# One product over 128 array rows for two terms of each output row, in a 3x3 convolution

## The chip, the cores and the metric

The kernel runs on one core of one Trainium2 chip. The metric is the device time of one execution in microseconds (us); lower is better. Three runs of the kernel before gave 126.46, 126.80 and 128.12 us, so the median is 126.8 us.

## What is computed

A 3x3 convolution with padding 1 over 16 images of 64 channels and 64x64 pixels, to 128 output channels. The weights are masked so that some nine in ten are zero, but the kernel does not use that.

```python
batch, c_in, h, w, c_out, k = 16, 64, 64, 64, 128, 3
x_pad = np.pad(x, ((0, 0), (0, 0), (1, 1), (1, 1)))
for b, co, ci, kh, kw:
    output[b, co] += weight[co, ci, kh, kw] * x_pad[b, ci, kh:kh+h, kw:kw+w]
```

`x` and `weight` are float32 in HBM, and so is the output (33.55 MB). The kernel multiplies in bfloat16 and sums in float32.

## The kernel before

**The arithmetic.** Two output rows, an even row 2r and the odd row 2r+1, share one product. Call the four input rows that they need d0 to d3, and the three rows of the filter g0, g1, g2, each of which stands for its three columns kw. The even row is g0·d0 + g1·d1 + g2·d2, the odd row g0·d1 + g1·d2 + g2·d3. The kernel computes

- P = g1·(d1 + d2), used by both rows,
- E = (g2 - g1)·d2 + g0·d0, so that the even row is P + E,
- O = (g0 - g1)·d1 + g2·d3, so that the odd row is P + O.

**Tiling.** Two images form a pair p (8 pairs). The 64 channels of the first image lie in partitions 0 to 63 and those of the second in 64 to 127. A pair is cut into four blocks of 16 output rows, which makes 32 blocks b; a block has eight even and eight odd rows of both images. A product takes one filter term, one column kw and one image n: it contracts over the 64 partitions of that image and gives 128 output channels by 8 rows by 64 columns (512 elements, or 504 where kw clips the edge). P has 3 columns x 2 images = 6 such matmuls, E and O have 2 terms x 3 columns x 2 images = 12 each, so a block has 30 (L292).

**What each engine does per block.**

- GpSimd (POOL) adds neighbouring rows, `ss` = d1 + d2, a 128x512 tile (L178). It also issues the loads of `x` (L134), which convert to bfloat16 on the way into `xs`.
- ScalarE (ACT) copies the 18 rows that a block needs from `xs` into the window `win` (L211; one 128x1152 copy), and evicts P from PSUM into `pcs` (L219).
- TensorE (PE) runs P, E and O of the block in that order. P waits for `ss` and for `win`; E waits until VectorE has taken the E of the block before out of `ps_e`, and O likewise with `ps_o`.
- VectorE (DVE) adds P + E and P + O into the output tile `os` (L248), two 128x1024 float32 instructions.
- SyncE (SP) stores a finished pair, 4 MB, and the last pair in two halves of 2 MB (L118, L124).

`win`, `ss`, `pcs` and the PSUM tile of P exist twice; `ps_e` and `ps_o` once; the output tile three times. The order of instructions on each engine is the order of the loops that are written out for it, with semaphores between engines (`s`: `ss` ready; `x`: window ready; `p`: P done; `q`: E or O done; `c`: ACT's copies; `e`, `o`: VectorE's sums; `r`: VectorE's marks).

**Head.** Weights are cast into `w_bf`, turned by nine matmuls against an identity (L267), and copied or subtracted into `wT`, which holds five filter rows: g0, g1, g2, g2 - g1, g0 - g1. Seven idle matmuls of 128 rows come before that and seven after it (L262). The first 32 rows of pair 0 arrive as float32 in `x_head`.

Of the kernel before, what the change touches and what calls it, by code (L numbers as in the profile page):

```python
# [12 lines left out]
G0, G1, G2, G21, G01 = range(5)  # L13
# [4 lines left out]
def kernel(  # L18
# [5 lines left out]
):  # L24

# [27 lines left out]
    win = tiles(2, [128, 18, W], BF16, "win")  # L53
# [7 lines left out]
    w_bf = pool.tile([C_OUT, 3, 4 * C_IN], BF16, name="w_bf")  # L61
    wT = pool.tile([128, 5, 3, C_OUT], BF16, name="wT")
# [24 lines left out]
    w_bf4 = w_bf.rearrange("o g (k i) -> o g k i", k=4)  # L87

    def cast_w(copy, g, a, b):
        k = 3 * g + a % 3  # L90
        return copy(out=w_bf4[:, g, a:b, :], in_=w_v[:, k : k + b - a, :])  # L91
# [5 lines left out]
    def tap(g, kw, n):  # L97
        return wT[64 * n : 64 * n + 64, g, (kw - n) % 3, :]

# [4 lines left out]
    HEAD_R, HEAD_C, HEAD_Q = 8, 4, 3  # L104
    R_OF = {p: HEAD_R + p + 1 for p in range(NP - 1)}

    with tc.tile_critical(no_gpsimd_drain=True):  # L107
        with nc.Block(no_gpsimd_drain=True) as block:  # L108
# [22 lines left out]
            def _(gp):  # L131
                def load(p, a, b, *waits):
# [5 lines left out]
                gp.memset(ident, 0.0).then_inc(S("s"), 1)  # L138
# [10 lines left out]
                    ("s", 1),  # L149
                ).then_inc(S("s"), 1)  # L150
# [13 lines left out]
                for b in range(NB):  # L164
                    p, r0 = b // 4, 16 * (b % 4)
                    waits = []
                    if b == 0:
                        waits.append(("xh", 16))
                    if b == 2 or (b % 4 == 0 and b):
                        waits.append((x_sem(p), X_LANDS[p]))  # L170
                    if b >= 2:
                        waits.append(("p", b - 1))
                    if b < 2:
                        src = x_head[:, r0 : r0 + 16, :]
                    else:
                        src = xs[:, p, r0 + 1 : r0 + 17, :]
                    after(
                        gp.tensor_tensor(  # L178
                            out=ss[b % 2], in0=src[:, 0:16:2, :], in1=src[:, 1:16:2, :], op=ADD
                        ),  # L180
                        *waits,
                    ).then_inc(S("s"), 1)
                    if b in AT:
                        load(*AT[b])

            @block.scalar
            def _(act):
                after(cast_w(act.copy, G1, 3, 4), ("w", 16)).then_inc(S("c"), 1)
                cast_w(act.copy, G2, 0, 3).then_inc(S("c"), 1)
                after(act.copy(out=wT[:, G1], in_=wps(G1)), ("q", 1)).then_inc(S("c"), 1)  # L190
                after(act.copy(out=wT[:, G2], in_=wps(G2)), ("q", 3)).then_inc(S("c"), 1)

                def window(b):
                    p, r0 = b // 4, 16 * (b % 4)
                    parts = [(xs[:, p, r0 : r0 + 18, :], 0, [])]
                    if b == 0:
                        parts = [(x_head[:, 0:17, :], 1, [("xh", 16)])]
                    elif b == 1:
                        parts = [
                            (x_head[:, 15:32, :], 0, []),  # L200
                            (xs[:, 0, 33:34, :], 17, [(x_sem(0), X_LANDS[0])]),
                        ]
                    elif b == 2:
                        parts = [(x_head[:, 31:32, :], 0, []), (xs[:, 0, 33:50, :], 1, [])]
                    elif b % 4 == 0:
                        parts[0][2].append((x_sem(p), X_LANDS[p]))
                    if b >= 2:
                        parts[0][2].append(("q", HEAD_Q + 2 * (b - 2) + 2))
                    for k, (src, a, waits) in enumerate(parts):
                        copy = after(  # L210
                            act.copy(out=win[b % 2][:, a : a + src.shape[1], :], in_=src), *waits  # L211
                        )
                        if k == len(parts) - 1:
                            copy.then_inc(S("x"), 1)

                window(0)
                window(1)
                for b in range(NB):
                    after(act.copy(out=pcs[b % 2], in_=ps_p[b % 2]), ("p", b + 1)).then_inc(S("c"), 1)  # L219
                    if b + 2 < NB:  # L220
                        window(b + 2)

            @block.vector
            def _(dve):
                dve.memset(idle_rhs, 0.0).then_inc(S("r"), 1)  # L225
                dve.memset(xs[:, :, 0 : H + 2 : H + 1, :], 0.0)
                dve.memset(win[0][:, 0:1, :], 0.0).then_inc(S("r"), 1)
                after(cast_w(dve.tensor_copy, G1, 0, 3), ("w", 16)).then_inc(S("r"), 1)
                cast_w(dve.tensor_copy, G0, 0, 3)
                cast_w(dve.tensor_copy, G0, 3, 4).then_inc(S("r"), 1)  # L230
                cast_w(dve.tensor_copy, G2, 3, 4).then_inc(S("r"), 1)
                after(dve.tensor_copy(out=wT[:, G0], in_=wps(G0)), ("q", 2)).then_inc(S("r"), 1)  # L232
                after(
                    dve.tensor_tensor(out=wT[:, G01], in0=wps(G0), in1=wT[:, G1], op=SUB), ("c", 3)
                ).then_inc(S("r"), 1)
                after(
                    dve.tensor_tensor(out=wT[:, G21], in0=wps(G2), in1=wT[:, G1], op=SUB), ("c", 4)
                ).then_inc(S("r"), 1)
                for b in range(NB):
                    p, r0 = b // 4, 16 * (b % 4)  # L240
                    for k, src in enumerate((ps_e, ps_o)):
                        waits = [("q", HEAD_Q + 2 * b + k + 1)]
                        if k == 0:
                            waits.append(("c", HEAD_C + b + 1))
                            if b % 4 == 0 and p >= N_O:
                                waits.append((f"st{p % N_O}", 16 * (p // N_O)))
                        after(
                            dve.tensor_tensor(  # L248
                                out=os[p % N_O][:, :, r0 + k : r0 + 16 : 2, :], in0=src, in1=pcs[b % 2], op=ADD
                            ),  # L250
                            *waits,
                        ).then_inc(S("eo"[k]), 1)
                    if b % 4 == 3 or b == NB - 3:
                        dve.memset(mark, 0.0).then_inc(S("r"), 1)

            @block.tensor
            def _(pe):
# [7 lines left out]
                def transposed(g, *waits):  # L265
                    for j in range(3):
                        mm = pe.matmul(  # L267
                            wps(g)[:, j, :], w_bf[:, g, C_IN * j : C_IN * (j + 2)], ident, start=True, stop=True
                        )
                        if j == 0:  # L270
                            after(mm, *waits)
                        if j == 2:
                            mm.then_inc(S("q"), 1)

                keep_busy(7, ("r", 1))
                pe.wait_ge(S("s"), 2)
                pe.sem_inc(S("s"), -2)
                transposed(G1, ("r", 3), ("c", 1))
                transposed(G0, ("r", 4))
                transposed(G2, ("r", 5), ("c", 2))  # L280
# [3 lines left out]
                pe.wait_ge(S("r"), HEAD_R)  # L284

                def product(dst, terms, name, waits):
                    todo = [(t, kw) for t in terms for kw in KW_ORDER]
                    for i, ((src, g, first, step), kw) in enumerate(todo):
                        c_lo, c_hi = max(0, 1 - kw), min(W, W + 1 - kw)
                        for n in range(2):  # L290
                            q = slice(64 * n, 64 * n + 64)
                            mm = pe.matmul(  # L292
                                dst[:, n, :, c_lo:c_hi],
                                tap(g, kw, n),
                                src[q, first : first + 7 * step + 1 : step, c_lo + kw - 1 : c_hi + kw - 1],
                                start=(i == 0),
                                stop=(i == len(todo) - 1),
                            )
                            if n == 0 and i == 0:
                                after(mm, *waits)  # L300
                            if n == 1 and i == len(todo) - 1:
                                mm.then_inc(S(name), 1)

                with pe.Fori(0, NB // TURN, 1):
                    for l in range(TURN):
                        xw = win[l]
                        product(ps_p[l], [(ss[l], G1, 0, 1)], "p", [("s", l + 1), ("x", l + 1)])
                        product(ps_e, [(xw, G21, 2, 2), (xw, G0, 0, 2)], "q", [("e", l + 1)])
                        product(ps_o, [(xw, G01, 1, 2), (xw, G2, 3, 2)], "q", [("o", l + 1)])
                    for name in ("s", "x", "e", "o"):  # L310
                        pe.sem_inc(S(name), -TURN)
# [36 lines left out]
```

## Time and profile before

The profiled execution took 126.21 us in all; the span in its trace is 124.4 us, so 1.81 us lie around the span.

| | us | share of the span |
|---|---|---|
| profiled execution | 126.21 | |
| its span | 124.4 | |
| PE busy | 109.6 | 88% |
| PEld (weight loads) busy | 49.1 | 39% |
| DVE busy | 79.2 | 64% |
| ACT busy | 69.3 | 56% |
| POOL busy | 43.0 | 35% |
| HBM traffic, read and written | 17.07 MB and 33.55 MB | 407 GB/s over the span |

A matmul's busy time overlaps that of its neighbours, so "PE busy" says that something was in the array, not that it was at its peak. PEld is TensorE's loading of weights. In the groups of instructions the columns are: line, engine, operation, output<-input, shape and count, then busy time in us and mean ns of one instruction, then the engine's idle time before them with what ended most of it.

### The profile page before, as it was taken

What the parts mean: (1) busy time and instruction counts of PE and PEld (TensorE: products, weight loads), DVE (VectorE), ACT (ScalarE), POOL (GpSimd) and SP (SyncE); (2) the same over time, 40 slices, a digit from 0 to 9 for tenths busy, and PEclk for the clock granted to TensorE, in tenths of its full rate; (3) what the DMA queues carried; (4) which work ended last, traced back from release to release, by engine and by line L of the source; (5) the groups of instructions that cost most, each with busy time, mean ns of one, the idle gap of its engine ahead of it and who ended that gap; (6) DMA issues with size and microseconds to landing.
All of it is one profiled execution on the core that took longest, in us unless ns stands there. A gap on an engine that the chain in (4) does not pass through costs nothing.

```text
span 124.4 us, 2437 instructions
## 1 busy us (share of the span) xinstructions
PE 109.6 (88%) x983; PEld 49.1 (39%) x983; DVE 79.2 (64%) x83; ACT 69.3 (56%) x71; POOL 43.0 (35%) x48
## 2 busy tenths in 40 slices
PE   5949999999999999999999999999999999992000
PEld 1414444444444444444444444444444444440000
DVE  2615676777677777777777767775867677775000
ACT  4564666666666666666666666657566666630000
POOL 5564333533353334433343334333333333000000
PEclk9999999999999999999999999999999999999855
DMA  3999999999999999999999999999999999999991
GB/s 85 375 225 213 211 219 219 239 438 338 332 363 432 308 329 324 387 353 345 298 379 408 321 369 427 413 367 348 433 421 432 427 384 427 458 390 416 413 419 71
DMA packets 4179, 42.79 MB, mean 344 GB/s; under 512 B 336, under 2 KB 336, under 8 KB 1104
## 3 DMA queue, kind: packets, MB, share of 16 engines
q1 hardware_dynamic: 2736, 34.90, 67.3%
q0 software_dynamic: 1440, 7.86, 30.6%
q14 instruction: 3, 0.02, 0.0%
HBM read 17.07 MB, written 33.55 MB: 407 GB/s over the span
## 4 chain that ended last, share of the span: by engine, by line
PE 84%; DMA 5%; POOL 1%; DVE 1%; SPq 0%; issue 0%; DVEq 0%
PE ps_e L292 33%; PE ps_o L292 33%; PE ps_p L292 17%; DMA x_head<-in_x_dram 5%; POOL s L178 1%; DVE o L248 1%; SPq L112 0%; SPq L343 0%; SPq L107 0%; DVEq L108 0%
## 5 line engine op out<-in xcount | busy, mean ns | idle before, releaser
L248 DVE TENSOR_TENSOR o<-ps_e,pc 128x1024 f32<-128x1024 f32 x32 | 39.2, 1225 | 31.2 <-ACT pc L219 22.9
L178 POOL TENSOR_TENSOR s<-xs 128x512 bf16<-128x512 bf16 x30 | 34.5, 1150 | 58.0 <-PE ps_p L292 58.0
L211 ACT COPY win<-xs 128x1152 bf16<-128x1152 bf16 (+2 forms) x31 | 34.7, 1121 | 34.2 <-PE ps_o L292 34.2
L292 PE MATMUL ps_e<-win,wT 64*128 64x504 bf16 (+1 forms) x384 | 46.8, 377 | 0.0
L292 PE MATMUL ps_o<-win,wT 64*128 64x504 bf16 (+1 forms) x384 | 46.8, 377 | 0.0
L248 DVE TENSOR_TENSOR o<-ps_o,pc 128x1024 f32<-128x1024 f32 x32 | 38.9, 1216 | 0.1
L219 ACT COPY pc<-ps_p 128x1024 f32<-128x1024 f32 x32 | 32.2, 1006 | 1.8 <-PE ps_p L292 1.8
L292 PEld LDWEIGHTS ps_o<-win,wT 64*128 64x128 bf16 x384 | 18.9, 94 | 22.6 <-DVE o L248 0.2
L292 PEld LDWEIGHTS ps_e<-win,wT 64*128 64x128 bf16 x384 | 18.8, 94 | 22.8 <-DVE o L248 0.8
L292 PE MATMUL ps_p<-s,wT 64*128 64x504 bf16 (+1 forms) x192 | 26.0, 377 | 1.6 <-POOL s L178 1.6
L292 PEld LDWEIGHTS ps_p<-s,wT 64*128 64x128 bf16 x192 | 9.4, 94 | 13.2 <-POOL s L178 2.1
L262 PE MATMUL ps_p<-idle_rhs 128*128 128x512 bf16 x14 | 4.8, 503 | 1.4 <-DVE idle_rhs L225 1.4
L134 POOL DMA_DIRECT2D xs<-in_x_dram x10 | 5.7, 573 | 1.0 <-SPq L107 1.0
L211 ACT CAST win<-x_head 128x1088 bf16<-128x1088 f32 (+1 forms) x3 | 2.3, 811 | 2.8 <-PE ps_o L292 1.6
L178 POOL TENSOR_TENSOR s<-x_head 128x512 bf16<-128x512 f32 x2 | 2.5, 1270 | 2.4 <-DMA x_head<-in_x_dram 2.4
L262 PEld LDWEIGHTS ps_p<-idle_rhs 128*128 128x128 bf16 x14 | 1.5, 117 | 3.4 <-DVE idle_rhs L225 1.4
L91 DVE CAST w_bf<-w_sb 128x192 bf16<-128x192 f32 (+1 forms) x4 | 1.1, 348 | 2.0 <-DMA w_sb<-in_weight_dram 2.0
L91 ACT ACT_TABLE_LOAD x1 | 1.3, 1283 | 0.9 <-SPq L107 0.9
L91 ACT CAST w_bf<-w_sb 128x64 bf16<-128x64 f32 (+1 forms) x2 | 0.7, 415 | 1.7 <-DMA w_sb<-in_weight_dram 1.7
L225 DVE MEMSET idle_rhs<- 128x256 uint32 x1 | 0.3, 272 | 1.1 <-SPq L107 1.1
L232 DVE CAST wT<-ps_e 128x384 bf16<-128x384 f32 x1 | 0.6, 557 | 0.3 <-PE ps_e L267 0.3
L190 ACT CAST wT<-ps_o 128x384 bf16<-128x384 f32 x1 | 0.5, 478 | 0.3 <-PE ps_o L267 0.3
(18 smaller groups left out, 5.4 us busy)
## 6 DMA issues: line engine op xcount, KB each, us to landing
out_dram<-o SPq DMA_DIRECT2D x7, 4096.0 KB, 17.3
xs<-in_x_dram POOLq DMA_DIRECT2D x5, 1024.0 KB, 16.3
out_dram<-o SPq DMA_DIRECT2D x2, 2048.0 KB, 10.3
xs<-in_x_dram POOLq DMA_DIRECT2D x3, 512.0 KB, 13.4
x_head<-in_x_dram SPq DMA_DIRECT2D x1, 1024.0 KB, 5.8
xs<-in_x_dram POOLq DMA_DIRECT2D x1, 640.0 KB, 14.2
xs<-in_x_dram POOLq DMA_DIRECT2D x1, 384.0 KB, 21.2
w_sb<-in_weight_dram SPq DMA_DIRECT2D x1, 288.0 KB, 2.9
```

The costliest lines, as they stand in the source:

```text
L91: return copy(out=w_bf4[:, g, a:b, :], in_=w_v[:, k : k + b - a, :])
L134: gp.dma_start(out=xs[:, p, a + 1 : b + 1, :], in_=pair(p)[:, a:b, :]), *waits
L178: gp.tensor_tensor(out=ss[b % 2], in0=src[:, 0:16:2, :], in1=src[:, 1:16:2, :], op=ADD),
L190: after(act.copy(out=wT[:, G1], in_=wps(G1)), ("q", 1)).then_inc(S("c"), 1)
L211: act.copy(out=win[b % 2][:, a : a + src.shape[1], :], in_=src), *waits
L219: after(act.copy(out=pcs[b % 2], in_=ps_p[b % 2]), ("p", b + 1)).then_inc(S("c"), 1)
L225: dve.memset(idle_rhs, 0.0).then_inc(S("r"), 1)
L232: after(dve.tensor_copy(out=wT[:, G0], in_=wps(G0)), ("q", 2)).then_inc(S("r"), 1)
L248: dve.tensor_tensor(out=os[p % N_O][:, :, r0 + k : r0 + 16 : 2, :], in0=src, in1=pcs[b % 2], op=ADD),
L262: mm = pe.matmul(idle_ps, idle_rhs[:, 0:128], idle_rhs, start=True, stop=True)
L292: mm = pe.matmul(dst[:, n, :, c_lo:c_hi], tap(g, kw, n), src[q, first : first + 7 * step + 1 : step, c_lo + kw - 1 : c_hi + kw - 1], start ...
```

## The change

E is now one product per column and image over all 128 partitions instead of two over 64: the window of image n holds d0 in one half of the partitions and, in the other half, the rows two further down, so that the array itself adds g0·d0 + (g2 - g1)·d2. O works in the same way, with (g0 - g1)·d1 and g2·d3. P stays as it was, in pairs of 64-row matmuls. A block has 6 + 6 + 6 = 18 matmuls.

`win[l]` becomes 128 x 2 images x 16 rows x 64, and is filled by four copies of 64 partitions x 1024 per block (`fill`; `upper` names the half of the partitions that is written, n the image):

- GpSimd: image 0, lower half
- VectorE: image 0, upper half (the source lies in partitions 0 to 63, the destination in 64 to 127)
- ScalarE: image 1, lower half (from 64 to 127 into 0 to 63) and image 1, upper half

E's first image now waits for the copies of GpSimd and VectorE, its second for both of ScalarE; P no longer waits for a window. On GpSimd the copy stands between the block's row sum and the load that may follow; on VectorE behind the two sums of the block two earlier; on ScalarE around the eviction of P.

In the head, `wT` holds three sets instead of five; the differences are taken when the weights are cast, and two subtractions from PSUM go. The row sums of blocks 0 and 1 move from GpSimd to VectorE.

```diff
-    win = tiles(2, [128, 18, W], BF16, "win")
+    win = tiles(2, [128, 2, 16, W], BF16, "win")
...
+    def fill(copy, b, n, upper, name):
+        p, r0 = b // 4, 16 * (b % 4)
+        src = slice(64 * n, 64 * n + 64)
+        dst = slice(64 * upper, 64 * upper + 64)
+        first = r0 - 1 + 2 * upper
...
+            if b >= 2 and k == 0:
+                waits.append(("q", HEAD_Q + 2 * (b - 2) + 2))
+            inst = after(copy(out=win[b % 2][dst, n, q : q + rows.shape[1], :], in_=rows), *waits)
+            if k == len(parts) - 1:
+                inst.then_inc(S(name), 1)
...
             @block.gpsimd
                 for b in range(NB):
...
+                    if b >= 2:
+                        waits = [("p", max(b - 1, 2))]
+                        if b == 2 or b % 4 == 0:
+                            waits.append((x_sem(p), X_LANDS[p]))
+                        after(row_sum(gp, b, xs[:, p, r0 + 1 : r0 + 17, :]), *waits).then_inc(S("s"), 1)
+                    fill(gp.tensor_copy, b, 0, 0, "xg")
                     if b in AT:
                         load(*AT[b])
...
             @block.scalar
-                window(0)
-                window(1)
+                fill(act.copy, 0, 1, 1, "xa")
+                fill(act.copy, 0, 1, 0, "xa")
+                fill(act.copy, 1, 1, 1, "xa")
                 for b in range(NB):
                     after(act.copy(out=pcs[b % 2], in_=ps_p[b % 2]), ("p", b + 1)).then_inc(S("c"), 1)
+                    if b + 1 < NB:
+                        fill(act.copy, b + 1, 1, 0, "xa")
                     if b + 2 < NB:
-                        window(b + 2)
+                        fill(act.copy, b + 2, 1, 1, "xa")
...
             @block.vector
+                for b in range(2):
+                    after(row_sum(dve, b, x_head[:, 16 * b : 16 * b + 16, :]), ("xh", 16)).then_inc(S("s"), 1)
+                    fill(dve.tensor_copy, b, 0, 1, "xd")
                 for b in range(NB):
...
+                    if b + 2 < NB:
+                        fill(dve.tensor_copy, b + 2, 0, 1, "xd")
...
             @block.tensor
+                    halves = [slice(64 * n, 64 * n + 64) for n in range(2)]
+                    if g == MID:
+                        order = [(kw, n, halves[n]) for kw in KW_ORDER for n in range(2)]
+                    else:
+                        order = [(kw, n, slice(0, 128)) for n in range(2) for kw in KW_ORDER]
...
-                        product(ps_p[l], [(ss[l], G1, 0, 1)], "p", [("s", l + 1), ("x", l + 1)])
-                        product(ps_e, [(xw, G21, 2, 2), (xw, G0, 0, 2)], "q", [("e", l + 1)])
-                        product(ps_o, [(xw, G01, 1, 2), (xw, G2, 3, 2)], "q", [("o", l + 1)])
+                        product(ps_p[l], lambda n: ss[l], MID, [[("s", l + 1)], []], "p")
+                        product(ps_e, lambda n: win[l][:, n, 0:16:2, :], EVEN,
+                            [[("e", l + 1), ("xg", l + 1), ("xd", l + 1)], [("xa", 2 * l + 2)]], "q")
+                        product(
+                            ps_o, lambda n: win[l][:, n, 1:16:2, :], ODD, [[("o", l + 1)], []], "q"
+                        )
```

More of the change, by code (lines that the diff above doesn't have):

```diff
@@ L11 @@
 SUB = mybir.AluOpType.subtract
-G0, G1, G2, G21, G01 = range(5)
+MID, EVEN, ODD = range(3)
 KW_ORDER = (1, 0, 2)
@@ L60 @@
     idle_rhs = pool.tile([128, 512], BF16, name="idle_rhs")
-    w_bf = pool.tile([C_OUT, 3, 4 * C_IN], BF16, name="w_bf")
-    wT = pool.tile([128, 5, 3, C_OUT], BF16, name="wT")
+    w_bf = pool.tile([C_OUT, 3, 3, 2, C_IN], BF16, name="w_bf")
+    wT = pool.tile([128, 3, 3, C_OUT], BF16, name="wT")
     mark = pool.tile([128, 1], FP32, name="mark")
@@ L86, with w_row @@
     w_v = w_sb.rearrange("o (i k) -> o k i", k=KH * KW)
[L87 to L91, printed above, removed]
+    def w_row(kh):
+        return w_v[:, 3 * kh : 3 * kh + 3, :]
     def wps(g):
@@ L95, in wps @@
         return flat[:, 0:384].rearrange("p (k c) -> p k c", k=3)
-    def tap(g, kw, n):
-        return wT[64 * n : 64 * n + 64, g, (kw - n) % 3, :]
     def x_sem(p):
@@ L103, with row_sum @@
     X_LANDS = {0: 16, 1: 16, 2: 16, 3: 16, 4: 32, 5: 32, 6: 32, 7: 48}
-    HEAD_R, HEAD_C, HEAD_Q = 8, 4, 3
+    HEAD_R, HEAD_C, HEAD_Q = 6, 5, 3
     R_OF = {p: HEAD_R + p + 1 for p in range(NP - 1)}
+    def row_sum(eng, b, rows):
+        return eng.tensor_tensor(out=ss[b % 2], in0=rows[:, 0:16:2, :], in1=rows[:, 1:16:2, :], op=ADD)
+    def fill(copy, b, n, upper, name):
[3 more added lines that the diff above has]
+        first = r0 - 1 + 2 * upper
+        parts = []
+        if p == 0 and first < HEAD:
+            a, z = max(first, 0), min(first + 16, HEAD)
+            parts.append((x_head[src, a:z, :], a - first))
+        if p or first + 16 > HEAD:
+            a, z = (first, first + 16) if p else (max(first, HEAD), first + 16)
+            parts.append((xs[src, p, a + 1 : z + 1, :], a - first))
+        for k, (rows, q) in enumerate(parts):
+            waits = []
+            if b == 0:
+                waits.append(("xh", 16))
+            if b == 1 and k == 1:
+                waits.append((x_sem(0), X_LANDS[0]))
+            if b and b % 4 == 0:
+                waits.append((x_sem(p), X_LANDS[p]))
[4 more added lines that the diff above has]
+                inst.then_inc(S(name), 1)
     with tc.tile_critical(no_gpsimd_drain=True):
@@ L137, in _ @@
                 load(0, HEAD, H)
-                gp.memset(ident, 0.0).then_inc(S("s"), 1)
+                gp.memset(ident, 0.0).then_inc(S("id"), 1)
                 after(
@@ L148, in _ @@
                     ),
-                    ("s", 1),
-                ).then_inc(S("s"), 1)
+                    ("id", 1),
+                ).then_inc(S("id"), 1)
                 for p in range(1, 4):
@@ L165, in _ @@
                     p, r0 = b // 4, 16 * (b % 4)
[L166 to L170, printed above, removed]
-                    if b >= 2:
[L172 to L182, printed above, removed]
+                    if b >= 2:
+                        waits = [("p", max(b - 1, 2))]
+                        if b == 2 or b % 4 == 0:
+                            waits.append((x_sem(p), X_LANDS[p]))
+                        after(row_sum(gp, b, xs[:, p, r0 + 1 : r0 + 17, :]), *waits).then_inc(S("s"), 1)
+                    fill(gp.tensor_copy, b, 0, 0, "xg")
                     if b in AT:
@@ L187, in _ @@
             def _(act):
[L188 to L214, printed above, removed]
@@ L216, in _ @@
-                window(0)
-                window(1)
+                after(act.copy(out=w_bf[:, MID, :, 1, :], in_=w_row(1)), ("w", 16)).then_inc(S("c"), 1)
+                act.copy(out=w_bf[:, EVEN, :, 0, :], in_=w_row(0)).then_inc(S("c"), 1)
+                act.copy(out=w_bf[:, ODD, :, 1, :], in_=w_row(2)).then_inc(S("c"), 1)
+                after(act.copy(out=wT[:, MID], in_=wps(MID)), ("q", 1)).then_inc(S("c"), 1)
+                after(act.copy(out=wT[:, ODD], in_=wps(ODD)), ("q", 3)).then_inc(S("c"), 1)
@@ L226, in _ @@
                 dve.memset(xs[:, :, 0 : H + 2 : H + 1, :], 0.0)
[L227 to L238, printed above, removed]
+                dve.memset(win[0][0:64, :, 0:1, :], 0.0).then_inc(S("r"), 1)
+                after(dve.tensor_copy(out=w_bf[:, MID, :, 0, :], in_=w_row(1)), ("w", 16)).then_inc(S("r"), 1)
+                for g, half, a, b in ((EVEN, 1, 2, 1), (ODD, 0, 0, 1)):
+                    dve.tensor_tensor(
+                        out=w_bf[:, g, :, half, :], in0=w_row(a), in1=w_row(b), op=SUB
+                    ).then_inc(S("r"), 1)
+                after(dve.tensor_copy(out=wT[:, EVEN], in_=wps(EVEN)), ("q", 2)).then_inc(S("r"), 1)
+                for b in range(2):
+                    after(row_sum(dve, b, x_head[:, 16 * b : 16 * b + 16, :]), ("xh", 16)).then_inc(S("s"), 1)
+                    fill(dve.tensor_copy, b, 0, 1, "xd")
                 for b in range(NB):
@@ L265, in transposed @@
                 def transposed(g, *waits):
[L266 to L270, printed above, removed]
+                    for kw in range(3):
+                        src = w_bf[:, g, kw].rearrange("o h i -> o (h i)")
+                        mm = pe.matmul(wps(g)[:, kw, :], src, ident, start=True, stop=True)
+                        if kw == 0:
                             after(mm, *waits)
-                        if j == 2:
+                        if kw == 2:
                             mm.then_inc(S("q"), 1)
                 keep_busy(7, ("r", 1))
[L276 to L280, printed above, removed]
+                pe.wait_ge(S("id"), 2)
+                transposed(MID, ("r", 3), ("c", 1))
+                transposed(EVEN, ("r", 4), ("c", 2))
+                transposed(ODD, ("r", 5), ("c", 3))
                 keep_busy(7)
@@ L284, in _ @@
                 pe.wait_ge(S("r"), HEAD_R)
-                def product(dst, terms, name, waits):
-                    todo = [(t, kw) for t in terms for kw in KW_ORDER]
-                    for i, ((src, g, first, step), kw) in enumerate(todo):
-                        c_lo, c_hi = max(0, 1 - kw), min(W, W + 1 - kw)
[L290 to L302, printed above, removed]
+                pe.wait_ge(S("c"), HEAD_C)
@@ new lines, in product @@
+                def product(dst, src, g, waits, name):
+                    halves = [slice(64 * n, 64 * n + 64) for n in range(2)]
[3 more added lines that the diff above has]
+                        order = [(kw, n, slice(0, 128)) for n in range(2) for kw in KW_ORDER]
+                    for i, (kw, n, q) in enumerate(order):
+                        c_lo, c_hi = max(0, 1 - kw), min(W, W + 1 - kw)
+                        mm = pe.matmul(
+                            dst[:, n, :, c_lo:c_hi],
+                            wT[q, g, kw, :],
+                            src(n)[q, :, c_lo + kw - 1 : c_hi + kw - 1],
+                            start=(kw == KW_ORDER[0]),
+                            stop=(kw == KW_ORDER[-1]),
+                        )
+                        if kw == KW_ORDER[0]:
+                            after(mm, *waits[n])
+                        if i == 5:
+                            mm.then_inc(S(name), 1)
@@ L304, in _ @@
                 with pe.Fori(0, NB // TURN, 1):
                     for l in range(TURN):
-                        xw = win[l]
-                        product(ps_p[l], [(ss[l], G1, 0, 1)], "p", [("s", l + 1), ("x", l + 1)])
-                        product(ps_e, [(xw, G21, 2, 2), (xw, G0, 0, 2)], "q", [("e", l + 1)])
-                        product(ps_o, [(xw, G01, 1, 2), (xw, G2, 3, 2)], "q", [("o", l + 1)])
-                    for name in ("s", "x", "e", "o"):
-                        pe.sem_inc(S(name), -TURN)
+                        product(ps_p[l], lambda n: ss[l], MID, [[("s", l + 1)], []], "p")
@@ new lines, in _ @@
+                        product(
+                            ps_e,
+                            lambda n: win[l][:, n, 0:16:2, :],
+                            EVEN,
+                            [
+                                [("e", l + 1), ("xg", l + 1), ("xd", l + 1)],
+                                [("xa", 2 * l + 2)],
+                            ],
+                            "q",
+                        )
+                        product(
+                            ps_o, lambda n: win[l][:, n, 1:16:2, :], ODD, [[("o", l + 1)], []], "q"
+                        )
@@ L313 @@
+                    for name, n in (("s", 1), ("xa", 2), ("xd", 1), ("xg", 1), ("e", 1), ("o", 1)):
+                        pe.sem_inc(S(name), -n * TURN)
     sixteen = nc.sync.to_reg(16)
```

## The prediction

> **What bounds the kernel now.** I read the chain of waits first. It is TensorE without a break, from 8.59 to 112.65 us; one block reads:
>
> ```profile
> 60.63 0.65 PE ps_p L292 x6
> 61.28 1.30 PE ps_e L292 x12
> 62.58 1.30 PE ps_o L292 x12
> 63.87 0.65 PE ps_p L292 x6
> ```
>
> (start, length, what). A block takes 63.87 - 60.63 = 3.24 us, and 32 of them 103.7. The costliest groups say what one matmul is:
>
> ```profile
> L292 PE MATMUL ps_e<-win,wT 64*128 64x504 bf16 (+1 forms) x384 | 46.8, 377 | 0.0
> ...
> L219 ACT COPY pc<-ps_p 128x1024 f32<-128x1024 f32 x32 | 32.2, 1006 | 1.8 <-PE ps_p L292 1.8
> ...
> L292 PEld LDWEIGHTS ps_e<-win,wT 64*128 64x128 bf16 x384 | 18.8, 94 | 22.8 <-DVE o L248 0.8
> ```
>
> Each lasts 377 ns, but 30 fit into 3.24 us, 108 ns apiece: the two images' 64-row matmuls run side by side, a pair every 3.24/15 = 216 ns. The groups between 5.3 and 7.1 us, then the timeline, show what one full-height matmul costs, by the idle ones of the head:
>
> ```profile
> L262 PE MATMUL ps_p<-idle_rhs 128*128 128x512 bf16 x7 | 1.7, 379 | 0.0
> L262 PEld LDWEIGHTS ps_p<-idle_rhs 128*128 128x128 bf16 x7 | 0.6, 98 | 0.6
> ```
>
> ```profile
> 5.32 1.67 PE L262 MATMUL ps_p<-idle_rhs 128*128 128x512 bf16 x7
> ```
>
> Seven in 1.67 us, the last lasting 0.379: (1.67 - 0.379)/6 = 215 ns each. So a 128-row matmul costs what a pair of 64-row ones costs.
>
> Last the end. The stores' time to landing from 107 us on, and their issues in the timeline:
>
> ```profile
> 113.95 0.37 SPq L124 DMA_DIRECT2D out_dram<-o  x1
> ```
>
> ```profile
> DMA to landing us min/median/max: 9.5/10.3/11.1
> ```
>
> From 113 us on the only store left takes 9.5, so the last half lands at 113.95 + 9.5 = 123.5, and the half issued at 107.53 at 107.53 + 11.1 = 118.6. The last 2.1 MB land 4.9 us after the half before, 430 GB/s, the rate of the last slices of the page (413 to 458). So the last store queued: the DMA engines are a second bound. The HBM line adds up to 17.07 + 33.55 = 50.6 MB, 117.7 us at 430 GB/s, of a 124.4 us span with busy share 9 in nearly every slice. Nothing that only shortens PE's work can take out much over 2 us.
>
> **The change part by part.**
>
> *Matmuls.* Before: 15 pairs x 216 ns. After: 3 pairs of P, and 12 of 128 rows at 215. Again 3.24 us. The 12 fewer matmuls save nothing.
>
> *Weight loads.* 18 per block instead of 30, of 94 or 98 ns. The idle matmuls carry one each at a pitch of 215, so a 128-row load hides under the matmul before: 0. The Trainium skill ("TensorE: Matmul & The Clock Gate", The mechanism) says that a load overlaps a running matmul only where the row groups differ. By that rule the idle pitch would hold the 98 ns too, which the 215 contradicts; the row decides, and the rule is the last rival.
>
> *Going between 64 and 128 rows.* This is new: P to E and O to P, twice a block, 64 times (the first P follows a gap). Inside the loop of before every matmul has 64 rows, and no dense sequence in the trace mixes heights, so it must be bounded. Low: 0, what a change of weights and bank costs now; a gain is excluded because the array accepts no more columns per time in either form (216 and 215). High: the array empties and the next load waits too, 377 - 216 + 98 = 259 ns. Between: it empties but the load hides, 377 - 216 = 161 ns. I take 161: in a pair the two halves of the array work on different matmuls, in a 128-row one on the same, so one may have to be done with before the other begins, and 161 is what the trace has for a matmul whose end nothing overlaps. 2 x 0.161 = 0.32 us a block, 10.3 in 32. The Trainium skill ("TensorEngine Tiling (Array Packing)", Key Properties) states that changing the tiling mode drains TensorE, and gives no price; no run here shows it.
>
> *ACT.* The 1152-element window copy goes (1.15 us; with 1088 elements 1.09, so 0.92 ns per element), two of 1024 come, about 1.03 each. Successive copies start some 0.09 earlier than they end (60.67 + 1.15, next at 61.73), so a block is 2 x 0.94 + 1.01 = 2.9 of 3.24 us. Queue: fill of b+2 at O's end, P's eviction, fill of b+1. The eviction is ready 0.1 us sooner than now. Cost 0; cover left 0.3 us.
>
> *DVE.* 2.43 of 3.24 us busy; it adds a 64x1024 bf16 copy between two SBUF tiles, which the trace lacks. Low: MEMSET of 128x512 words, the same bytes, 0.485. High: the 128x1024 sum from PSUM, 1.225. I take 0.485, nearest in memory and bytes: 2.92, hidden. At 1.225 with overlaps of 0.08 it is 3.42, and 0.18 x 32 = 5.8 us show. Queued behind it is the next P + E sum, which idles 0.8 to 0.9 us for P's eviction today, and behind that the next E, which needs `ps_e`.
>
> *POOL.* 1.15 us a block; it adds a 1024-element copy. Low 1.15 (the row sum reads 2 x 512), high 2.3 (it writes 512): 2.3 or 3.45 us. I take 1.15, for the elements read: hidden. The loads behind the copy are issued some 2.6 us later (after O of two blocks back instead of P); they land 20 us or more before use, so 0.
>
> *Head.* `ss` of block 0 moves to DVE: the 384-element sum took 0.55, so 512 some 0.65 to 0.7 against 1.28, and P starts 0.6 us earlier. But ACT now has four copies (1024, 960, 960, 64 elements, about 2.9 us) before it evicts P of block 0, near 10.1 instead of 9.45; the sum ends near 12.4, and E of block 1 starts there instead of 12.65. Net gain 0.2, and hidden by the queue of stores. Two subtractions fewer end before `x_head` lands at 7.2: 0.
>
> *Sum.* PE ends at 112.65 + 10.3 = 122.95; the sum and issue take 113.95 - 112.65 = 1.3; the last store goes out at 124.25. Alone it needs 4.9 us plus a start: the 0.29 MB of weights took 2.9 from issue to landing, 0.7 of it at 430 GB/s, so 2.2. It lands at 131.35 rather than 123.5: the queue of today, 9.5 - 7.1 = 2.4 us, absorbs part. With 124.4 - 123.5 = 0.9 of span behind it and the 1.81 around the span: 134.1 us, against the profiled 126.21 (0.6 below the median of the runs).
>
> **The rivals.** *Not slower: the change of height is free* or costs little. For it: the pair and the single matmul have the same pitch, and each product's first matmul today changes weights, bank and waits without a bubble. Against: the trace has never seen the two mixed. PE then ends where it did, and DMA ends the span: 126.2. It decides below the point where 2% (2.5 us) show behind the 2.4 of queue: 4.9/64 = 77 ns. Bounds 125.6 (the head's 0.6) to 128.7.
>
> *A helper takes over the bound.* DVE at 1.225: 126.2 + 5.8 - 2.4 = 129.6. POOL at 2.3: 3.45 - 3.24 = 0.21 x 32 = 6.7, so 130.5. Or the two hold each other up: POOL starts its copy at O's end and the next row sum 1.15 later, so DVE's copy, wanted 1.3 after O's end behind P + O, would wait for 2.3, end at 2.8, and the next sum at 4.0, against E's start at 3.89: 0.1 x 32 = 3.5, so 127.3. For it: DVE and ACT lose most of their spare time; against: all the nearest rows fit. That a VectorE copy in a two-port mode and a GpSimd instruction shut each other out is in the Trainium skill ("SBUF — State Buffer", Who interferes with whom); no run here shows it.
>
> *The weights' loads show*: 12 x 98 ns x 32 = 37.6 - 2.4, 161 us. The idle matmuls speak against it.
>
> *Faster by over 2%*: 123.7 or less. Only if stores overlap better than now; the busy share leaves no room.
>
> **How the numbers follow.** Changes of height over 77 ns: 46 in 100 (forecast, 134.1; its own range 129 to 140.4, the latter at 259 ns: 16.6 - 2.4). Free or cheaper: 37. A helper: 12, of which 2 stay inside 2%. Loads: 1. Faster: 4. So faster 0.04, same 0.39, slower 0.57; the 2% stand for what a measurement of this kernel can tell from no change. The range has to reach both: from 125.6, the low bound of the free case, to 136 (190 ns a change), leaving out some 15.
>
> **What would show it.** In the chain of the changed kernel, a block of 3.56 us, with a gap of some 0.16 in front of each first P and first E matmul, and the last store landing 7 us after issue: forecast. Blocks of 3.24 and the last store still in a queue: free. E's idle ended by DVE or POOL copies: helper. The forecast is wrong if P, E and O follow one another at 0.65, 1.30 and 1.30 us.

## The result, and the profile after

The changed kernel takes 133.34 us (median of 4 runs, 133.25 to 136.69) against 126.63 of the kernel before on the same chip: a ratio of 1.050, with a 95% interval of 1.041 to 1.059. The forecast was 134.1, slower. Some executions of a kernel stand a few per cent above the rest, here the highest of the four; ratios leave them out, and where a profile below is of one (experiments 1 and 2), its extra time lies ahead of the second block. Its profiled execution took 133.27 us, with a span of 131.5: 7.1 us more than before.

The chain of waits, first in a stretch where TensorE is alone on it, then around one where it is not (start, length, what):

```profile
96.24 0.75 PE ps_p L289 x6
97.00 1.40 PE ps_e L289 x6
98.40 1.30 PE ps_o L289 x6
99.69 0.75 PE ps_p L289 x6
```

```profile
69.54 0.71 DVE win L129
70.26 0.95 issue
71.21 1.24 DVE o L242
72.44 0.05 issue
72.49 1.47 PE ps_e L289 x6
```

A block takes 99.69 - 96.24 = 3.45 us instead of 3.24. P went from 0.65 to 0.75 and E from 1.30 to 1.40, O kept its 1.30: a piece holds the gap in front of it, so the loss stands in front of P and in front of E, where 64 and 128 rows meet. In the second stretch E waits for VectorE's sum, and that sum for VectorE's own copy into the window.

The costliest groups among the new and altered ones, with busy time and mean ns, then idle time in front:

```profile
L129 ACT COPY win<-xs 64x1024 bf16<-64x1024 bf16 (+2 forms) x61 | 62.7, 1028 | 13.7 <-PE ps_o L289 13.7
L129 POOL COPY win<-xs 64x1024 bf16<-64x1024 bf16 (+1 forms) x30 | 30.8, 1027 | 34.0 <-PE ps_o L289 34.0
...
L129 DVE COPY win<-xs 64x1024 bf16<-64x1024 bf16 (+1 forms) x31 | 31.0, 1000 | 0.9
...
L289 PEld LDWEIGHTS ps_p<-s,wT 64*128 64x128 bf16 x192 | 6.8, 94 | 17.8 <-issue 12.7
```

ScalarE's copy is what the forecast took (1.03), GpSimd's is a little under its low bound (1.03 for 1.15), VectorE's is twice what it took (1.00 for 0.485). The last line is the change of height from the side of the weight loads: 12.7 us in which P's first loads waited for nothing that the profile shows, 0.42 us in each of 30 blocks, of which 0.12 is the usual gap between two loads (216 - 98 ns).

The end of the kernel, by stages: the columns are the stretch, its length, then each engine's busy time and count, the granted clock, the DMA engines' busy share and GB/s.

```profile
100.00:106.80 6.80, 6.80 (x40) 2.55 (x36) 6.67 (x6) 5.88 (x7) 4.18 (x5) 1.00 0.91 386
106.80:109.30 2.50, 2.50 (x16) 1.01 (x13) 2.43 (x5) 2.48 (x3) 2.01 (x2) 1.00 0.00 0
109.30:111.00 1.70, 1.70 (x12) 0.49 (x11) 1.70 (x2) 1.26 (x2) 0.88 (x1) 1.00 0.72 308
111.00:130.00 19.00, 9.41 (x48) 3.55 (x46) 9.26 (x11) 6.09 (x7) 2.29 (x3) 0.87 0.99 414
```

For 2.5 us the DMA engines have nothing to do: in the kernel before the stores always queued here (a share of 0.96 to 1.00 from 88 to 114 us), now the queue runs dry in front of the store of pair 6. That store goes out at 109.25 and takes 11.3 us to land; the two halves of the last pair follow it at 4.9 us each, since each is issued (at 115.5 and 121.7) while the store before it is still under way. 109.25 + 11.3 + 2 x 4.9 = 130.4, and the span ends at 131.5.

### The profile page after: what moved, and what is told of

The parts are those of the page before. It is cut to its first block, busy times and chain, and to the rows that moved or that the text cites. A ratio compares the mean times of both kernels' runs of the same rounds, so it can differ in the third digit from the quotient of the medians.

```text
span 131.5 us, 1819 instructions
## 1 busy us (share of the span) xinstructions
PE 116.9 (89%) x599; PEld 43.9 (33%) x599; DVE 113.7 (86%) x115; ACT 99.5 (76%) x104; POOL 74.0 (56%) x79
## 4 chain that ended last, share of the span: by engine, by line
PE 40%; DVE 27%; issue 12%; ACT 9%; DMA 4%; SPq 0%; DVEq 0%
DVE o L242 19%; PE ps_e L289 17%; PE ps_o L289 16%; DVE win L129 8%; PE ps_p L289 7%; ACT win L129 6%; DMA x_head<-in_x_dram 4%; ACT pc L213 2%; SPq L138 0%; SPq L350 0%; DVEq L242 0%; SPq L133 0%; DVEq L134 0%
## 5 line engine op out<-in xcount | busy, mean ns | idle before, releaser
L129 ACT COPY win<-xs 64x1024 bf16<-64x1024 bf16 (+2 forms) x61 | 62.7, 1028 | 13.7 <-PE ps_o L289 13.7
L129 POOL COPY win<-xs 64x1024 bf16<-64x1024 bf16 (+1 forms) x30 | 30.8, 1027 | 34.0 <-PE ps_o L289 34.0
L289 PE MATMUL ps_e<-win,wT 128*128 128x504 bf16 (+1 forms) x192 | 47.0, 381 | 1.6 <-DVE o L242 1.0
L289 PE MATMUL ps_o<-win,wT 128*128 128x504 bf16 (+1 forms) x192 | 46.8, 380 | 0.0
L129 DVE COPY win<-xs 64x1024 bf16<-64x1024 bf16 (+1 forms) x31 | 31.0, 1000 | 0.9
L289 PEld LDWEIGHTS ps_e<-win,wT 128*128 128x128 bf16 x192 | 16.2, 97 | 30.8 <-DVE o L242 11.1
L289 PEld LDWEIGHTS ps_o<-win,wT 128*128 128x128 bf16 x192 | 18.8, 98 | 22.7 <-DVE o L242 0.6
L289 PEld LDWEIGHTS ps_p<-s,wT 64*128 64x128 bf16 x192 | 6.8, 94 | 17.8 <-issue 12.7
L129 ACT CAST win<-x_head 64x1024 bf16<-64x1024 f32 (+2 forms) x5 | 4.3, 861 | 0.7 <-DMA x_head<-in_x_dram 0.6
L129 POOL CAST win<-x_head 64x960 bf16<-64x960 f32 (+2 forms) x3 | 3.4, 1141 | 2.3 <-DMA x_head<-in_x_dram 2.3
```

The costliest lines, as they stand in the source:

```text
L129: inst = after(copy(out=win[b % 2][dst, n, q : q + rows.shape[1], :], in_=rows), *waits)
L289: mm = pe.matmul(dst[:, n, :, c_lo:c_hi], wT[q, g, kw, :], src(n)[q, :, c_lo + kw - 1 : c_hi + kw - 1], start=(kw == KW_ORDER[0]), stop=(k ...
```

## The experiments

Two theories from the first reading. "Height": each change between 64 and 128 rows costs TensorE a fixed time. "Helpers": the copies that were added on GpSimd, VectorE and ScalarE lengthen the block. The runs below take one away and leave the other. Times are medians; ratios are to the kernel before on the same chip, with 95% intervals.

### 1. The change of height alone

The kernel before, all other engines untouched. Only E and O are multiplied as in the changed kernel.

```diff
-                    todo = [(t, kw) for t in terms for kw in KW_ORDER]
...
+                    if tall:
+                        todo = [(terms[n], kw, n, slice(0, 128)) for n in range(2) for kw in KW_ORDER]
...
```

> The kernel before, with its window, its ScalarE copy and all its other engines untouched; only the 12 pairs of E and O become 12 matmuls of 128 rows, term 0 for the first image and term 1 for the second (the sums over the terms are left out, so that the number of array slots stays 15 a block). Theory 'height': each change between 64 and 128 rows costs TensorE some 106 ns, so a block takes 3.24 + 0.21 = 3.45 us with no further stall, PE ends near 112.6 + 6.7 = 119.3, the store of pair 6 goes out some 5.9 us later, and the time is about 131 us (ratio 1.035 to 1.04). Rival 'helpers': the added copies on GpSimd, VectorE and ScalarE are what lengthens the block; they are absent here, so the block stays at 3.24 and the time at 126.5.

Measured: 131.11 us, ratio 1.039 (1.035 to 1.043). The chain of waits of this run:

```profile
61.24 0.75 PE ps_p L294 x6
62.00 1.40 PE ps_e L294 x6
63.40 1.30 PE ps_o L294 x6
64.70 0.76 PE ps_p L294 x6
```

A block of 64.70 - 61.24 = 3.46 us with none of the copies. "Height" holds, and alone it is worth some 5 us.

### 2. The copies alone

The changed kernel with 64-row matmuls in pairs for E and O.

```diff
-                        order = [(kw, n, slice(0, 128)) for n in range(2) for kw in KW_ORDER]
+                        order = [(kw, n, halves[n]) for _ in range(2) for kw in KW_ORDER for n in range(2)]
...
```

> The changed kernel with all its copies, waits and its head, but E and O multiplied in pairs of 64-row matmuls as before (each image's own half of the partitions, twice; the other half's term is left out). Theory 'height': the block returns to 3.24 us, apart from stalls of 0.26 us in about one block of four where VectorE's copy comes behind GpSimd's; 126 to 127.5 us. Rival 'helpers': the copies are still there, so the block stays near 3.45 and the time near 133.

Measured: 131.2 us, ratio 1.038 (1.033 to 1.044). I had expected 126 to 127.5. So the copies alone cost as much as the changes of height alone. The timeline of this run (start, length, engine, line, operation) shows how:

```profile
63.23 0.42 DVE L129 COPY win<-xs 64x1024 bf16<-64x1024 bf16 x1
63.68 1.23 DVE L242 TENSOR_TENSOR o<-ps_e,pc 128x1024 f32<-128x1024 f32 x1
...
64.93 1.23 DVE L242 TENSOR_TENSOR o<-ps_o,pc 128x1024 f32<-128x1024 f32 x1
...
65.03 1.03 POOL L129 COPY win<-xs 64x1024 bf16<-64x1024 bf16 x1 [1.86 <-PE ps_o L289]
...
66.03 1.15 POOL L104 TENSOR_TENSOR s<-xs 128x512 bf16<-128x512 bf16 x1
...
66.19 1.27 DVE L129 COPY win<-xs 64x1024 bf16<-64x1024 bf16 x1
...
67.49 1.23 DVE L242 TENSOR_TENSOR o<-ps_e,pc 128x1024 f32<-128x1024 f32 x1
```

A VectorE copy takes 0.42 us when GpSimd is idle. The next one is recorded for 1.27: it starts while GpSimd's row sum runs (66.03 to 67.18) and ends 0.28 after that ends. VectorE's next sum, which frees `ps_e` for TensorE, waits behind it.

### 3. VectorE's copy made sixteen times smaller

```diff
+            if name == "xd" and b >= 2:
+                rows = rows[:, 0:1, :]
             inst = after(copy(out=win[b % 2][dst, n, q : q + rows.shape[1], :], in_=rows), *waits)
```

> The changed kernel with VectorE's copy cut to one row of 16 from block 2 on (the other 15 rows of that quarter of the window keep what they held). Theory 'height plus lock': the block stays at 3.45 us, the five stalls of 0.26 us at E go, since VectorE no longer waits a GpSimd instruction out for 0.4 us of its own copying; PE ends 1.3 us earlier, 132 us. Rival 'VectorE's copy is the larger part': 128 us or less. Rival 'no lock': the stalls stay, 133.3.

Measured: 131.7 us, ratio 1.044 (1.039 to 1.048). The block stays at 3.45, and the stalls of 0.26 shrink to 0.02 to 0.07. The timeline of VectorE and of GpSimd in this run:

```profile
61.56 1.02 DVE L131 COPY win<-xs 64x64 bf16<-64x64 bf16 x1
62.61 1.22 DVE L244 TENSOR_TENSOR o<-ps_e,pc 128x1024 f32<-128x1024 f32 x1
```

```profile
60.40 1.03 POOL L131 COPY win<-xs 64x1024 bf16<-64x1024 bf16 x1 [1.40 <-PE ps_o L291]
61.39 1.14 POOL L104 TENSOR_TENSOR s<-xs 128x512 bf16<-128x512 bf16 x1
```

A copy of 64 elements is recorded for 1.02 us, and it ends just as the row sum ends (61.39 + 1.14 = 62.53). Its length is not its work but GpSimd's instruction. The Trainium skill says as much ("SBUF — State Buffer", Who interferes with whom): a VectorE copy in a two-port mode and a GpSimd instruction exclude each other for a whole instruction, and the one that comes second waits. The traces agree for a copy that starts during a row sum: 0.42 us alone, 1.27 where it had to wait the row sum out. That the copy runs in such a mode no run here shows. Below, this waiting is called the lock.

### 4. The copies without the lock

GpSimd's row sum waits until VectorE's copy is done, so that the two don't meet. Here with the paired matmuls of the second experiment:

```diff
                         fill(dve.tensor_copy, b + 2, 0, 1, "xd")
+                        dve.memset(mark_g[:, b : b + 1], 0.0).then_inc(S("g"), 1)
...
+                        if b >= 3:
+                            waits.append(("g", b - 2))
                         after(row_sum(gp, b, xs[:, p, r0 + 1 : r0 + 17, :]), *waits).then_inc(S("s"), 1)
```

> As the run with all copies and 64-row pairs (E and O: each image's own half twice, the other half's term left out), but GpSimd's row sum of a block waits until VectorE's copy for the block before it is done (a mark of one element tells it), so that the copy meets no GpSimd instruction. Theory 'lock': what lengthened that run to 131.2 us is VectorE's copy standing still while GpSimd's row sum runs; here the copies take 0.42 us each, the stalls of 0.17 and 0.70 at E go, blocks take 3.24, and the time is 126 to 127.5 us. Rival 'the work itself': ScalarE's two copies or VectorE's added work bound the block, the time stays at 130 or more.

Measured: 127.54 us, ratio 1.011 (1.002 to 1.019). VectorE's copies in the groups of this run:

```profile
L130 DVE COPY win<-xs 64x1024 bf16<-64x1024 bf16 x30 | 13.3, 445 | 0.9
```

445 ns instead of 959 in the second experiment, for the same 30 copies, and every block from the third on takes 3.24. The lock is all that the helpers cost in the loop; ScalarE's two copies and VectorE's own work fit. The time lies at the upper end of the 126 to 127.5 us that I expected: TensorE ends at 112.8 us, where it ended at 112.6 in the kernel before, but the last store lands 0.9 us later.

### 5. The changed kernel without the lock

> The changed kernel with that same wait of GpSimd's row sum for VectorE's copy; it computes the same as the changed kernel. Theory 'two bounds side by side': the five stalls of 0.26 us go and nothing else, the block stays at 3.45 us through the changes of height; 131.3 to 132 us. Rival 'the lock was the larger part': 129 or less.

The same edit on the changed kernel. Measured: 132.01 us, ratio 1.045 (1.038 to 1.052). All blocks after the first take 3.45. The four kernels of one construction then stand like this:

| ratio to the kernel before | pairs of 64 rows | 64 and 128 rows |
|---|---|---|
| row sum after the copy, no lock | 1.011 | 1.045 |
| as the change has it, lock | 1.038 | 1.050 |

Against the first cell the changes of height add 0.034, the lock 0.027, and both together 0.039, not 0.061. (The intervals of 1.045 and 1.050 overlap; that the lock still costs something beside the changes of height is seen in the traces, where the five stalls are gone.) They lie side by side and not behind each other: VectorE's late sum delays E only by what remains when TensorE has lost its 0.21 us a block anyway.

### 6. More and fewer changes of height

Four changes a block, in the kernel before (O in three pairs, then three 128-row matmuls; 15 slots of 216 ns as ever, a pair or a 128-row matmul in each):

```diff
+                    else:
+                        todo = [(terms[0], kw, n, halves[n]) for kw in KW_ORDER for n in range(2)]
+                        todo += [(terms[1], 1, 0, tall), (terms[1], 0, 1, tall), (terms[1], 2, 0, tall)]
...
```

> The kernel before with only its matmuls altered, to four changes of height a block and the same 15 slots: P in pairs, E in six 128-row matmuls, O in three pairs and then three 128-row matmuls (the sums are not those of the convolution). Theory 'height': the price is per change and adds up, 4 x 0.106, so a block takes 3.24 + 0.42 = 3.67 us, PE ends near 126, and the time is about 136.5 us. Rival 'the price hangs on the product (its new bank and waits), not on the height': 3.45 us as with two changes, 131.

Measured: 137.35 us, ratio 1.085 (1.077 to 1.093), and in its chain a block of 64.10 - 60.44 = 3.66 us:

```profile
60.44 1.40 PE ps_e L300 x6
61.84 1.51 PE ps_o L300 x9
63.35 0.76 PE ps_p L300 x6
64.10 1.40 PE ps_e L300 x6
```

O, with one change in front of it and one inside, has 1.51 in place of 1.30. The price is per change and adds up.

P from the lower 64 rows alone, unpaired, in the kernel of the first experiment:

```diff
-                        todo = [(terms[0], kw, n, slice(64 * n, 64 * n + 64)) for kw in KW_ORDER for n in range(2)]
+                        todo = [(terms[0], kw, n, slice(0, 64)) for n in range(2) for kw in KW_ORDER]
```

> The kernel before with E and O as 128-row matmuls, and P as six single matmuls on the lower 64 rows alone (the second image's P is computed from the first image's half). Theory 'height': what costs is the change of height, not the pairing; P takes 6 x 216 = 1.30 instead of 0.65 us and the two changes their 0.21, so a block takes 3.24 + 0.65 + 0.21 = 4.10 us. Rival 'only pairs need the array to be clear': 3.89.

And P over all 128 rows, so that no height changes:

```diff
+                        todo = [(terms[0], kw, n, slice(0, 128)) for n in range(2) for kw in KW_ORDER]
```

> The same with P as six matmuls over all 128 rows (the sum of both images instead of each). Theory 'height': no change of height is left, so nothing is lost between products and a block takes 3.24 + 0.65 = 3.89 us. Rival 'the price is that of a new product (bank, waits, weights)': 4.10.

Measured, one run each: 150.95 us with a block of 4.10, and 143.82 with a block of 3.89. The chains, first 64 rows, then 128:

```profile
62.30 1.40 PE ps_p L294 x6
63.70 1.40 PE ps_e L294 x6
65.10 1.30 PE ps_o L294 x6
```

```profile
63.06 1.30 PE ps_p L294 x6
64.36 1.30 PE ps_e L294 x6
65.65 1.30 PE ps_o L294 x6
```

With one height throughout, each product takes its 6 x 216 ns, although bank, weights and waits change as before. So neither a new product nor the pairing costs anything; the change of height does, in both directions. The Trainium skill's rule ("TensorEngine Tiling (Array Packing)", Key Properties), that a change of tiling mode drains TensorE while a change of tile does not, agrees with the traces in which changes cost something; it gives no price, and here it is 0.106 us. That the array drains is not shown by them.

### 7. Half the changes of height: a miss

P of two blocks behind one another, then E, O, E, O, with a third buffer for P's eviction.

```diff
-    pcs = tiles(2, [128, 2, 8, W], FP32, "pc")
+    pcs = tiles(3, [128, 2, 8, W], FP32, "pc")
...
+                    product(ps_p[0], lambda n: ss[0], MID, [[("s", 1)], []], "p")
+                    product(ps_p[1], lambda n: ss[1], MID, [[("s", 2), ("xa", 2)], []], "p")
                     for l in range(TURN):
-                        product(ps_p[l], lambda n: ss[l], MID, [[("s", l + 1)], []], "p")
                         product(
                             ps_e,
```

> The changed kernel with P of two blocks computed one behind the other (P, P, E, O, E, O; a third buffer for P's eviction), so that there are two changes of height in two blocks instead of four; it computes the same. Theory 'height': two blocks take 6.91 - 0.21 = 6.70 us, PE ends some 3.3 us earlier, and the time falls to about 130 us (130 to 131 if the stalls of E stay). Rival 'helpers': the number of changes does not matter, 133.

Measured: 136.74 us, ratio 1.079 (1.070 to 1.087). I put that down to the lock and took it away as in the fourth experiment:

> The run with P of two blocks behind one another, with that same wait; it computes the same as the changed kernel. Theory 'two bounds side by side': that run gained nothing from half the changes of height because the lock held VectorE's copy, and with it E; with the lock out of the way two blocks take 6.48 + 0.21 = 6.70 us instead of 6.89 to 7.23, and the time falls from 136.7 to 128 to 130 us (its head loses some 2 us, since P of block 1 waits for a second row sum). Rival 'the order itself is bad': 133 or more.

Measured: 136.40 us, ratio 1.076 (1.069 to 1.084), two blocks in 6.89 us where the changed kernel takes 2 x 3.45. That theory fell as well. The waits in the timeline of this last run:

```profile
63.76 1.46 PE L293 MATMUL ps_o<-win,wT 128*128 128x512 bf16 x6
63.96 1.23 DVE L245 TENSOR_TENSOR o<-ps_e,pc 128x1024 f32<-128x1024 f32 x1 [0.80 <-PE ps_e L293]
65.24 0.98 PEld L293 LDWEIGHTS ps_e<-win,wT 128*128 128x128 bf16 x6 [0.52 <-DVE o L245]
```

With no P between O and the next E, TensorE comes back to `ps_e` after one product of 1.30 us, and VectorE's sum out of that single buffer takes 1.23 plus its start: E begins 0.05 after the sum ends at 65.19. P was what covered that. The 0.2 us that two changes fewer save in two blocks are given back there. In addition the first two blocks take 10.57 us, against 4.16 + 3.45 in the changed kernel. P of block 1 now waits for the second row sum before any E runs; and from 11.4 to 14.8 us TensorE's granted clock is 0.50 in this trace (1.00 from there to 110 us), so that P of block 1 and E of block 0 take 1.40 and 2.16 us where 0.75 and 1.31 are usual. That makes 1.5 us of the miss. All four runs of this kernel have a mean granted clock of 0.951 to 0.962, against 0.971 to 0.976 in three of the four of the changed kernel; whether the order of the products brings the low clock about is not shown.

### 8. The mark behind the copy

In the changed kernel VectorE sets the mark that releases a pair's store after its copy, not after the pair's last sum. Moved ahead:

```diff
+                    if b % 4 == 3 or b == NB - 3:
+                        dve.memset(mark, 0.0).then_inc(S("r"), 1)
                     if b + 2 < NB:
                         fill(dve.tensor_copy, b + 2, 0, 1, "xd")
-                    if b % 4 == 3 or b == NB - 3:
-                        dve.memset(mark, 0.0).then_inc(S("r"), 1)
```

> The changed kernel with the mark that releases a pair's store put ahead of VectorE's copy instead of behind it; it computes the same. Theory 'mark': in the changed kernel the mark comes 1.06 us after the last sum of a pair, because the copy (0.42 us and its wait for GpSimd) stands before it, and the end hangs on the store of pair 6 (issued 109.26, 11.3 us on the way, then two halves of 4.9 each); so 1.0 to 1.1 us less, about 132.2. Rival 'the stores queue anyway': 133.3.

Measured: 132.5 us, ratio 1.044 (1.039 to 1.050) after 1.050 (1.041 to 1.059), some 0.8 us less by the ratios. The intervals overlap, so the sign is as expected and the size not settled. With both repairs:

> The changed kernel with both repairs, the row sum after VectorE's copy and the mark ahead of it; it computes the same. By the run with the first repair alone (132.0) less the 0.5 us by which the mark still comes late there: 131.5. What is left above the kernel before is then the changes of height, about 5 us. Rival: if the time falls below 130, the changes of height are not what is left.

Measured: 131.78 us, ratio 1.039 (1.031 to 1.046), which can't be told from the 1.045 with the first repair alone. It equals the 1.039 of the first experiment, in which nothing but the height of E and O was altered: within these intervals, what remains is the changes of height. None of the versions beats the kernel before.

## Why the prediction was right

The direction, the bound and the first cause were right, and 134.1 against 133.3 is close. The terms behind the sum were less so: two of them were wrong against each other, and that the sum came so close is in part luck.

- *Matmuls, weight loads.* Right. 128-row matmuls run at 216 ns one behind another (six in 1.30 us with one height throughout), with their loads hidden.
- *Going between 64 and 128 rows.* That each change costs TensorE a fixed time, in front of P and of E, was right. The size was off: 0.106 us a change (in the changed kernel the seven blocks from 92.79 to 116.96 us take 3.453 each; less 3.24, halved) for the 0.161 that I took as the end of a matmul that nothing overlaps. So 64 changes cost 6.8 us of TensorE's time, not 10.3. And the picture behind the 0.161, an array that empties while the next load hides, is not what the trace shows around a change:

```profile
60.80 0.38 PE L289 MATMUL ps_o<-win,wT 128*128 128x504 bf16 x1
61.11 0.33 PEld L289 LDWEIGHTS ps_p<-s,wT 64*128 64x128 bf16 x6 [0.42 <-issue]
61.11 0.82 PE L289 MATMUL ps_p<-s,wT 64*128 64x512 bf16 x6
```

  P's first weight load is not taken ahead: it starts together with its matmul, and TensorE's queue had waited for nothing visible. P's first matmul is recorded even before the last one of O ends (60.80 + 0.38 = 61.18), but the ends of matmuls are modelled. One load lasts 0.094 to 0.098 us, so a load that nothing covers would account for nearly all of the 0.106; whether it is that or an array that empties, no run here tells apart.
- *VectorE.* The copy's own cost was right (0.42 for 0.485). That it stands still behind GpSimd's row sum I had only as a rival, at 0.1 us a block. In the changed kernel it shows as five stalls of 0.26 us, 1.3 us in all: each in a block in which GpSimd issues one of its five loads in the loop. The issue takes 0.57 us and puts the row sum that much later, and the copy waits for the end of both:

```profile
69.13 0.57 POOL L160 DMA_DIRECT2D xs<-in_x_dram  x1
...
69.54 1.63 DVE L129 COPY win<-xs 64x1024 bf16<-64x1024 bf16 x1
69.72 1.16 POOL L104 TENSOR_TENSOR s<-xs 128x512 bf16<-128x512 bf16 x1
```

  By the record the copy starts 0.18 us before the row sum here, so it isn't merely the second to come; but it starts while the load is being issued. In the run of the fifth experiment such a copy meets the issue and no row sum, and takes 0.55 us instead of 0.42: the issue seems to hold it too, and the row sum then goes first. I had priced those loads at 0, by looking only at when their data is needed.
- *The rival "the change of height is free"* was priced wrong: with free changes the time would not have gone back to 126.2 but to the 131 of the second experiment, because the lock was the next bound, nearly as near as the first. The twelve per cent for helpers were too few in that sense. The mechanism that came true, VectorE and GpSimd holding each other up, was among them at 0.1 us a block and 127.3 us; the second experiment shows 0.17 and 0.70 in every four blocks, some 0.22 a block, and 131.2 us.
- *ACT, POOL.* Right: without the lock their copies are hidden, in blocks of 3.24 us (fourth experiment).
- *Head.* P of block 0 starts 0.8 us earlier, as forecast and a little more, but the first block then takes 4.16 us instead of 3.25: E of block 0 waits 0.7 us for VectorE's conversion of 1024 elements from `x_head`, recorded for 1.36 where the next, of 960, has 0.66. A loss of 0.1 instead of a gain of 0.2.
- *Sum.* TensorE ends 7.8 us later: 6.5 for the changes of height after the first block, stalls 1.3, head and first block 0.1, less 0.1 for a single stall that the kernel before has. The queue of stores absorbed 0.7 of it in the span, not 2.4. The step that failed there is that I reckoned the tail from the last half alone: the store of pair 6 decides, it found the DMA engines idle, and 8.4 MB go out behind its issue. It also came 1.06 us later than its pair's last sum, because the mark that releases it had moved behind VectorE's copy; that edit I did not see. The forecast's 10.3 less 2.4 is 7.9, the measured 7.8 less 0.7 is 7.1: TensorE's loss was put 2.5 us too high and the queue's help 1.7 too high, and only the luck that one nearly cancels the other brings 134.1 so close to 133.3.

## What to carry to other kernels

Two half-height matmuls side by side took the same 216 ns as one of full height: to join them saves nothing, and where both heights are used in turn, each change costs about 0.1 us. So count the changes, and keep longer stretches at one height if that opens no new wait, as it did in the seventh experiment. Before a copy is given to VectorE as spare work, look at what GpSimd does in the same microsecond; the order of the two engines can be worth more than the copy. And price a rival with the first cause taken away: here two bounds of nearly the same size lay side by side, and a repair of either alone would have shown little.

## What the runs showed of the hardware that was not expected

VectorE's copies of 64 elements per partition were recorded for 966 ns on average (27 of them; one that meets nothing takes 167), so a recorded duration can be nearly all waiting, and an engine's busy share with it: 86% for VectorE in the changed kernel, 77% when the same work keeps out of the lock. And the change of height costs a lone 64-row matmul, whose other half of the array is idle, as much as a pair.
